# A batched fp32 matmul on one core: the last four batches by halves of the weights, transposes between matmuls, three stores behind the last load

## The chip, the cores and the metric

The kernel runs on one core of one Trainium2 chip. The metric is the device time of one execution in microseconds (us). The profile's span is about 1.8 us shorter than the time of the same execution (525.0 and 526.8 us for the kernel before).

## The reference

```python
def setup_inputs():
    batch, m, k, n = 32, 512, 1024, 768
    return {"x": randn(batch, m, k), "weight": randn(batch, k, n)}   # float32

def reference(x, weight):
    return np.matmul(x, weight).astype(np.float32)
```

Each of the 32 batches reads 2 MB of x and 3 MB of weights, and writes 1.5 MB.

## The kernel before

Engines have the profile's names: PE does the matmuls and the transposes (PEld is its weight loads), DVE is the vector engine, ACT the scalar engine, POOL is GpSimd. PSUM is the memory that PE writes to, and an "evacuation" is the copy of finished outputs from PSUM to SBUF, the core's other memory, from where they are stored. A transfer has "landed" when its semaphore says that it is complete. In the profile's lines x_sb and w_sb are tiles of x and of the weights, pt is a group of transposes in PSUM, xT its copy in SBUF, pm the products in PSUM and out_sb the outputs.

Loads go through GpSimd's queue and cast fp32 to bf16 on the way. PE transposes x (16 transposes of 128x128 pairs per batch, in four groups, one for each tile `mt` of 128 output rows), DVE copies the transposed tiles out of PSUM, and PE multiplies: 64 matmuls per batch, 8 rows of weight tiles (`ko`) times 4 tiles `mt` times 2 column pieces. Most outputs are stored by the Sync engine's queue as soon as they are ready. The parts that matter (cuts are marked `...`):

```python
    KT = K // P                                            # 8 rows of weight tiles
    ...
    N2 = 2 * N                                             # columns of a pair of tiles mt
    CHUNKED = {B - 2: (4, 4), B - 1: (3, 3, 1, 1)}         # load pieces of the last two batches
    HELD = {B - 3, B - 2}                                  # stores put behind the last load
    ...
    xT_pool = ctx.enter_context(tc.tile_pool(name="xT", bufs=6))
    tpsum = ctx.enter_context(tc.tile_pool(name="tpsum", bufs=2, space=bass.MemoryType.PSUM))
    ...
    def load_w(b):
        ws[b] = w_pool.tile([P, KT, N], BF16, name="w_sb")
        at = 0
        for n in CHUNKED.get(b, (KT,)):
            nc.gpsimd.dma_start(out=ws[b][:, at:at + n, :], in_=w_view[b, :, at:at + n, :])
            at += n
    ...
    def evacuate(b, pair, pm):                             # PSUM -> out_sb: 1.0 us ACT, then 0.7 us DVE
        o = outs[b]
        nc.scalar.copy(o[:, pair * N2:pair * N2 + 1024], pm[:, 0:1024])
        nc.vector.tensor_copy(o[:, pair * N2 + 1024:(pair + 1) * N2], pm[:, 1024:N2])
    ...
        for b in range(B):
            if b + 4 < B:
                load_x(b + 4)
                load_w(b + 4)
            outs[b] = out_pool.tile([P, MT * N], F32, name="out_sb")
            if b not in CHUNKED:                           # the "ordinary" order
                xT = {mt: transpose(b, mt) for mt in (0, 1)}
                for pair in range(2):
                    pm = mpsum.tile([P, N2], F32, name="pm")
                    for half in range(2):
                        if pair == 0:
                            matmuls(pm, half, xT[half], b, range(KT), False)
                            xT[2 + half] = transpose(b, 2 + half)
                        else:
                            matmuls(pm, half, xT[2 + half], b, range(KT), False)
                    evacuate(b, pair, pm)
                if b in HELD:
                    continue
                nc.sync.dma_start(out_view[b], outs[b])
            else:                                          # all four transposes in front, then pieces of ko
                xT = {mt: transpose(b, mt) for mt in range(MT)}
                pms = [mpsum.tile([P, N2], F32, name="pm") for _ in range(2)]
                at = 0
                for n in CHUNKED[b]:
                    for mt in range(MT):
                        matmuls(pms[mt // 2], mt % 2, xT[mt], b, range(at, at + n), True)
                        if at + n == KT and mt % 2 == 1:
                            evacuate(b, mt // 2, pms[mt // 2])
                            ...                            # store the pair, unless b is in HELD
                    at += n
            if b == B - 2:
                for h in sorted(HELD):
                    nc.gpsimd.dma_start(out=out_view[h], in_=outs[h])
```

Batches are counted from 0, so the last is batch 31. A "group" of transposes below means the four transposes of one tile `mt`.

## Time and profile before

| | before |
|---|---|
| time, median of the 4 runs beside the changed kernel | 527.17 us (525.1 to 528.21) |
| span of the profiled run | 525.0 us |
| HBM traffic over the span | 415 GB/s |
| last load landed | 504.7 us |
| last matmul ended | 517.8 us |

From the page, the header and three rows of the 40 slices; each digit is a tenth of a slice of 13.1 us, and PEclk is the clock that PE was granted:

```profile
span 525.0 us, 5849 instructions
...
PE   1788879888789878789878798787998878997884
...
PEclk9999999889898989898979989898898989998998
DMA  8999999999999999999999999999999999999982
```

The DMA row is full until the last two slices: for most of the span the loads and stores set the pace, and PE has idle tenths. The last slices are another stage. Here is the chain of waits there (start us, length us, what; the chain is what ended last, followed back):

```profile
471.55 0.95 PE pt L64 x8
472.50 3.66 another core or an unknown queue
...
476.30 4.37 PE pm L78 x16
...
484.22 5.21 PE pm L78 x32
...
489.45 1.02 ACT out_sb L89
...
491.84 1.35 PE pt L64 x8
493.19 10.41 PE pm L78 x64
...
503.62 1.02 ACT out_sb L89
...
506.01 1.35 PE pt L64 x8
507.36 9.76 PE pm L78 x60
```

L78 is the matmul, L64 the transpose. Batch 29 waits 3.66 us for its weights (they land at 476.2; the chain calls the load "an unknown queue"). After that no load appears in the chain: batch 30 starts at 493.19 and batch 31 at 507.36, each after a stretch of about 3.76 us (489.43 to 493.19, 503.60 to 507.36) in which the evacuation, DVE and two rounds of transposes follow one another. PE is behind the loads, and the DMA engines run dry. The windows view shows that, with the two stretches around the wait for batch 29's weights on top. Behind each busy time stands the number of instructions (x); the GB/s count a cast load by its bf16 size (134.59 MB by that count, against 218.1 MB that the page gives for HBM):

```profile
core 0: us, PE busy (x) PEld busy (x) DVE busy (x) ACT busy (x) POOL busy (x), PEclk, DMA share, GB/s
...
472.50:476.20 3.70, 0.00 (x1) 0.00 (x0) 1.89 (x3) 0.10 (x1) 0.00 (x0) 1.00 0.99 214
476.20:479.60 3.40, 3.31 (x11) 1.60 (x12) 0.00 (x0) 0.00 (x0) 0.53 (x1) 0.50 1.01 304
...
505.00:510.00 5.00, 3.99 (x25) 2.80 (x26) 2.85 (x5) 0.00 (x0) 0.53 (x1) 1.00 0.83 347
510.00:515.00 5.00, 5.00 (x33) 3.04 (x32) 0.00 (x0) 0.00 (x0) 0.00 (x0) 1.00 0.15 61
515.00:520.00 5.00, 2.76 (x17) 1.46 (x15) 1.38 (x2) 1.93 (x2) 0.00 (x0) 1.00 0.06 26
```

The DMA share falls to 0.15 and 0.06 while PE still works, and only then are the last 1.5 MB stored. PE idles for 3.7 us from 472.5, and in the 3.4 us after it the granted clock is 0.50: 16 matmuls took 4.37 us there, against 2.60 at full speed.

### The profile page before, as it was taken

How to read it: one execution, taken by the hardware profiler on the slowest of the kernel's cores; microseconds unless marked ns; L12 is line 12 of the kernel's file. 1: busy time of each engine (PE TensorE's matmuls, PEld its weight loads, DVE VectorE, ACT ScalarE, POOL GpSimd, SP SyncE). 2: the span in 40 equal slices, each digit the busy share in tenths (PEclk: the TensorE clock that was granted, in tenths of full speed). 3: DMA queues.
4: the chain of work that ended last, by engine and by line, in shares of the span. 5: the costliest groups of instructions: out<-in, count | busy, mean ns of one | idle time of the engine just before them, and what ended most of it. 6: DMA issues, size and time to landing. Idle time of an engine off the chain costs nothing.

```text
span 525.0 us, 5849 instructions
## 1 busy us (share of the span) xinstructions
PE 431.3 (82%) x2560; PEld 279.3 (53%) x2560; DVE 123.9 (24%) x192; ACT 66.0 (13%) x65; POOL 37.8 (7%) x76
## 2 busy tenths in 40 slices
PE   1788879888789878789878798787998878997884
PEld 1455546555456545455545565454665545664552
DVE  1022221222221212221212212222222212222221
ACT  0001111011110111110101110101110101110011
POOL 4000000000000000000000000000000000000000
PEclk9999999889898989898979989898898989998998
DMA  8999999999999999999999999999999999999982
GB/s 160 215 228 272 271 268 271 277 253 259 263 260 278 261 278 246 265 261 277 262 273 231 273 274 271 274 246 265 258 273 275 254 270 243 274 275 272 214 294 122
DMA packets 14569, 134.59 MB, mean 256 GB/s; under 512 B 1616, under 2 KB 1872, under 8 KB 2640
## 3 DMA queue, kind: packets, MB, share of 16 engines
q0 software_dynamic: 10080, 87.04, 77.6%
q1 hardware_dynamic: 4464, 47.19, 21.7%
q8 instruction: 20, 0.33, 0.2%
q14 instruction: 5, 0.04, 0.0%
HBM read 167.77 MB, written 50.33 MB: 415 GB/s over the span
## 4 chain that ended last, share of the span: by engine, by line
PE 80%; another core or an unknown queue 11%; DMA 3%; ACT 2%; issue 2%; DVE 1%; ACTq 0%; POOL 0%; DVEq 0%; POOLq 0%
PE pm L78 70%; PE pt L64 10%; DMA w_sb<-in_weight_dram 3%; ACT out_sb L89 2%; DVE xT L66 1%; DVE out_sb L90 0%; ACTq L164 0%; POOL x_sb L50 0%; DVEq L66 0%; POOLq L153 0%
## 5 line engine op out<-in xcount | busy, mean ns | idle before, releaser
L78 PE MATMUL pm<-w_sb,xT 128*128 128x256 bf16 (+1 forms) x2048 | 377.0, 344 | 73.8 <-DMA w_sb<-in_weight_dram 63.5
L78 PEld LDWEIGHTS <-xT 128*128 128x128 bf16 x2048 | 208.0, 103 | 218.3 <-issue 61.5
L66 DVE COPY xT<-pt 128x1024 bf16<-128x1024 bf16 x128 | 85.1, 686 | 226.8 <-PE pt L64 226.8
L89 ACT COPY out_sb<-pm 128x1024 f32<-128x1024 f32 x64 | 64.7, 1013 | 452.3 <-PE pm L78 452.3
L64 PE MATMUL pt<-ident,x_sb 128*128 128x128 f32 x512 | 79.7, 291 | 12.6 <-DMA x_sb<-in_x_dram 9.7
L64 PEld LDWEIGHTS pt<-ident,x_sb 128*128 128x128 f32 x512 | 76.6, 207 | 19.8 <-issue 11.9
L90 DVE COPY out_sb<-pm 128x512 f32<-128x512 f32 x64 | 43.9, 686 | 169.1 <-ACT out_sb L89 169.1
L56 POOL DMA_DIRECT2D w_sb<-in_weight_dram x36 | 19.1, 531 | 241.2 <-DMA w_sb<-in_weight_dram 212.4
L50 POOL DMA_DIRECT2D x_sb<-in_x_dram x32 | 17.1, 536 | 198.7 <-PE pt L64 140.6
L138 POOL DMA_DIRECT2D out_dram<-out_sb x2 | 1.1, 534 | 28.1 <-DVE out_sb L90 28.1
L89 ACT ACT_TABLE_LOAD x1 | 1.3, 1283 | 0.7 <-PEq L153 0.7
masks.py:199 POOL TENSOR_SCALAR_AFFINE_SELECT ident<-ident 128x128 f32<-128x128 f32 x1 | 0.3, 287 | 0.1
masks.py:197 POOL MEMSET ident<- 128x128 f32 x1 | 0.2, 243 | 0.0
L153 POOL MEMSET const-float32-0.0<- 128x1 f32 x1 | 0.1, 99 | 0.2 <-issue 0.2
L153 POOL MEMSET const-bfloat16-1.0<- 128x1 bf16 x1 | 0.1, 102 | 0.0
L153 POOL MEMSET const-uint8-127<- 128x1 uint8 x1 | 0.1, 102 | 0.0
L153 POOL MEMSET const-float32-1.0<- 128x1 f32 x1 | 0.1, 99 | 0.0
## 6 DMA issues: line engine op xcount, KB each, us to landing
w_sb<-in_weight_dram POOLq DMA_DIRECT2D x30, 1536.0 KB, 63.1
out_dram<-out_sb SPq DMA_DIRECT2D x29, 1536.0 KB, 14.4
x_sb<-in_x_dram POOLq DMA_DIRECT2D x32, 1024.0 KB, 62.1
out_dram<-out_sb POOLq DMA_DIRECT2D x2, 1536.0 KB, 12.3
w_sb<-in_weight_dram POOLq DMA_DIRECT2D x2, 768.0 KB, 58.3
out_dram<-out_sb SPq DMA_DIRECT2D x2, 768.0 KB, 3.8
w_sb<-in_weight_dram POOLq DMA_DIRECT2D x2, 576.0 KB, 45.6
w_sb<-in_weight_dram POOLq DMA_DIRECT2D x2, 192.0 KB, 32.5
```

Source lines behind the costliest of these rows:

```text
L50: nc.gpsimd.dma_start(out=xs[b], in_=x_view[b])
L56: nc.gpsimd.dma_start(out=ws[b][:, at:at + n, :], in_=w_view[b, :, at:at + n, :])
L64: nc.tensor.transpose(pt[:, j, :], pairs[:, mt, j::JT], ident)
L66: nc.vector.tensor_copy(xT.rearrange("p j m r -> p (j m r)"), pt.bitcast(BF16).rearrange("p j m -> p (j m)"))
L78: nc.tensor.matmul(pm[:, half * N + off:half * N + off + size], xT[:, ko // 2, :, ko % 2], ws[b][:, ko, off:off + size], start=(ko == 0 an ...
L89: nc.scalar.copy(o[:, pair * N2:pair * N2 + 1024], pm[:, 0:1024])
L90: nc.vector.tensor_copy(o[:, pair * N2 + 1024:(pair + 1) * N2], pm[:, 1024:N2])
L138: nc.gpsimd.dma_start(out=out_view[h], in_=outs[h])
L153: nc = _bacc.Bacc("TRN2", target_bir_lowering=False, num_devices=1)
```

## The change

Its intent is to make PE's tail shorter and to use the DMA engines in it. Batches 28 to 31 are loaded and multiplied by halves of the weight rows (the last one by 4, 2, 2). In the second half of a batch, each tile's transposes for the next batch stand in front of that tile's matmuls. Batch 28's store joins the two that wait behind the last load in GpSimd's queue.

```diff
-    CHUNKED = {B - 2: (4, 4), B - 1: (3, 3, 1, 1)}
-    HELD = {B - 3, B - 2}
+    CHUNKED = {B - 4: (4, 4), B - 3: (4, 4), B - 2: (4, 4), B - 1: (4, 2, 2)}
+    HELD = {B - 4, B - 3, B - 2}
...
-    xT_pool = ctx.enter_context(tc.tile_pool(name="xT", bufs=6))
+    xT_pool = ctx.enter_context(tc.tile_pool(name="xT", bufs=8))
...
+        ready = {}
         for b in range(B):
...
-            else:
-                xT = {mt: transpose(b, mt) for mt in range(MT)}
...
+            xT = ready.pop(b, None) or {mt: transpose(b, mt) for mt in range(MT)}
+            pms = [mpsum.tile([P, N2], F32, name="pm") for _ in range(2)]
+            at = 0
+            for n in CHUNKED[b]:
+                last = at + n == KT
+                for mt in range(MT):
+                    if last and b + 1 < B:
+                        ready.setdefault(b + 1, {})[mt] = transpose(b + 1, mt)
+                    matmuls(pms[mt // 2], mt % 2, xT[mt], b, range(at, at + n), True)
+                    if last and mt % 2 == 1:
+                        pair = mt // 2
+                        evacuate(b, pair, pms[pair])
+                        if b not in HELD:
+                            cols = slice(pair * N2, (pair + 1) * N2)
+                            nc.sync.dma_start(out_view[b, :, cols], outs[b][:, cols])
+                at += n
+            if b in HELD:
+                nc.gpsimd.dma_start(out=out_view[b], in_=outs[b])
```

More of the change, by code (lines that the diff above doesn't have):

```diff
@@ L116 @@
                     evacuate(b, pair, pm)
-                if b in HELD:
-                    continue
                 nc.sync.dma_start(out_view[b], outs[b])
-            else:
-                xT = {mt: transpose(b, mt) for mt in range(MT)}
-                pms = [mpsum.tile([P, N2], F32, name="pm") for _ in range(2)]
-                at = 0
-                for n in CHUNKED[b]:
-                    for mt in range(MT):
-                        matmuls(pms[mt // 2], mt % 2, xT[mt], b, range(at, at + n), True)
-                        if at + n == KT and mt % 2 == 1:
-                            evacuate(b, mt // 2, pms[mt // 2])
-                            if b not in HELD:
-                                pair = mt // 2
-                                nc.sync.dma_start(
-                                    out_view[b, :, pair * N2:(pair + 1) * N2],
-                                    outs[b][:, pair * N2:(pair + 1) * N2],
-                                )
-                    at += n
-            if b == B - 2:
-                for h in sorted(HELD):
-                    nc.gpsimd.dma_start(out=out_view[h], in_=outs[h])
+                continue
+            xT = ready.pop(b, None) or {mt: transpose(b, mt) for mt in range(MT)}
[16 more added lines that the diff above has]
+                nc.gpsimd.dma_start(out=out_view[b], in_=outs[b])
 _INS = ['x', 'weight']
```

## The prediction

> **What bounds the kernel now.** Two things, in two stages. For most of the span it is the DMA engines: the slices show them at 9 tenths or more from slice 2 to 38, and the waits list 63.5 us of matmuls waiting for weight loads. The last 50 us differ. In the chain of waits, from the landing of batch 29's weights (476.2 us) to the last matmul (517.4), no load releases the chain: it is PE work, broken by two stretches of 3.7 us (from 489.4, from 503.6) in which the next batch's transposes go through two PSUM buffers and DVE. By the landing records the last weight piece arrives at 504.7. In the windows view the DMA share falls from 1.04 to 0.83 (505 to 510), 0.15 and 0.06 (515 to 520). So about 9 us of DMA time lie unused while PE catches up, and 1.5 MB must still be stored; the span ends 7.6 us after the last matmul.
>
> **What the change does.** Arithmetic and bytes stay.
> 1. Batch 28's store leaves the load stream. Batch 30's loads, with that store beside them, took 16.2 us (landings 476.1 to 492.3); batch 31's, with no store, 12.4. I expect the last load near 501.
> 2. Transposes go between the matmuls of the batch before: batches 29 to 31 lose their 3.6 us stretches and pay four groups of about 0.5 us (four transposes in the chain).
> 3. PE may start on half of the weights: batch 29, which waited until 476.3 for 1.5 MB, can start near 474, behind batch 28.
> 4. The clock records show 3.4 us at half speed from 476.2, just after PE idled from 472.5 to 476.3. The Trainium skill (TensorE: Matmul & The Clock Gate, Part 1) says that an idle window of about 3.4 us throttles PE; this trace agrees. With a dense tail this window, worth 1.7 us, should go.
> 5. The last batch's pair 0 finishes 1.3 us before pair 1, so its evacuations no longer queue: about 1 us.
>
> **Sum.** A batch costs PE 10.4 us of matmuls plus 2.0 of transposes. Batch 28 starts near 461 (its own transposes still stand in front), 29 at 474, 30 at 488 (x of batch 30 lands near 481 and holds its transposes 1.5 us), 31 at 500.5; last matmul near 511 instead of 517.4. Then evacuation 1.8, store issue to landing 4.3, closing 1.0: end near 518. The DMA side gives nearly that: three held stores behind the last load at 3.7 us each (batch 29's store landed 3.7 us after the last load) end near 512, then the last 1.5 MB.
>
> Savings 7 us of 527.36: **520.2 us**, 517.0 to 523.8 (8 in 10). Chances: faster by over 2% 0.09, within 2% 0.90, slower 0.01.
>
> **What would show it.** Chain of waits: no 3.7 us gaps in batches 29 to 31, last matmul near 511. Landings: last load near 501. Windows: DMA share about 1 up to 512. Clock records: no half-speed window between 461 and 511. If the last load lands at 504 or later, step 1 is wrong; if PE still idles over 2 us between batches, step 2 or 3 is.
>
> **What would make it wrong.** The held stores delaying the last 1.5 MB (then the end comes later than 6.5 us after the last matmul); loads in halves moving fewer bytes per us; x of batches 30 and 31 landing late and stopping PE where the transposes now stand.

## The result, and the profile after

| | before | changed |
|---|---|---|
| time, median | 527.17 us (4 runs) | 520.43 us (4 runs, 520.14 to 521.41) |
| ratio to before | | 0.988, 95% interval 0.9847 to 0.9913 |
| span of the profiled run | 525.0 | 518.8 |
| last load landed | 504.7 | 501.1 |
| last held store landed | 513.4 | 512.2 |
| last matmul ended | 517.8 | 512.1 |

A ratio is the mean time of one kernel's fast runs over the mean of the other's of the same rounds, so it is not quite the ratio of the medians quoted. The gain of 1.2% is clear of the noise.

The same rows of the page for the changed kernel, slices of 13.0 us:

```profile
span 518.8 us, 5796 instructions
...
PE   1788789788888878897888978788887879878994
...
PEclk9999899798998979998899989799898997998998
DMA  8999999999999999999999999999999999999996
```

The last slice of the DMA row has gone from 2 tenths to 6, and the one before is full. The chain of waits in the tail:

```profile
465.36 2.83 another core or an unknown queue
...
468.32 1.10 PE pt L64 x4
469.42 2.37 PE pm L78 x8
...
475.82 6.50 PE pm L78 x40
482.32 0.47 PE pt L64 x4
...
488.12 2.71 PE pm L78 x17
...
494.62 0.47 PE pt L64 x4
...
500.42 6.28 PE pm L78 x39
...
506.76 5.38 PE pm L78 x32
512.14 0.02 issue
512.16 1.02 ACT out_sb L89
```

The two stretches of 3.76 us are gone: a group of transposes costs PE 0.47 us between matmuls. A new wait stands at 465.36: in the middle of batch 28, PE waits for x of batch 29, whose transposes now come there; it lands at 468.2. The windows view of the same places:

```profile
core 0: us, PE busy (x) PEld busy (x) DVE busy (x) ACT busy (x) POOL busy (x), PEclk, DMA share, GB/s
465.40:468.30 2.90, 0.00 (x0) 0.01 (x1) 0.00 (x0) 0.00 (x0) 0.00 (x0) 0.96 1.04 327
468.00:471.40 3.40, 3.08 (x11) 1.93 (x12) 0.69 (x1) 0.00 (x0) 0.53 (x1) 0.51 1.05 237
505.00:510.00 5.00, 4.95 (x31) 3.04 (x31) 0.00 (x0) 0.00 (x0) 0.00 (x0) 1.00 0.87 369
510.00:515.00 5.00, 2.12 (x14) 1.08 (x12) 1.38 (x2) 2.02 (x2) 0.00 (x0) 1.00 0.41 168
```

The half-speed stretch has not gone; it has moved from batch 29 to batch 28, behind the new wait. The DMA share from 510 to 515 is 0.41 where it was 0.15.

An account of the 6.2 us between the two spans follows from these chains. Both kernels end batch 29 at the same time, 489.4 (in the changed kernel: 488.12 and eight matmuls of 0.163 us). But in the changed one batch 30's transposes are done by then. From there, before needs twice 3.76 and twice 10.4 us, until 517.8; the changed kernel needs 12.3 (10.4 and four groups of 0.47) and 10.4, until 512.1. That is 5.6 us less; the span then ends 6.7 us after the last matmul instead of 7.3, the other 0.6.

### The profile page after: what moved, and what is told of

Same layout as the page of the kernel before. It is cut to its first block, busy times and chain, and to the rows that moved or that the text cites. A ratio compares the mean times of both kernels' runs of the same rounds, so it can differ in the third digit from the quotient of the medians.

```text
span 518.8 us, 5796 instructions
## 1 busy us (share of the span) xinstructions
PE 425.6 (82%) x2512; PEld 278.3 (54%) x2560; DVE 124.2 (24%) x192; ACT 66.1 (13%) x65; POOL 38.9 (7%) x78
## 4 chain that ended last, share of the span: by engine, by line
PE 80%; another core or an unknown queue 10%; DMA 3%; issue 2%; ACT 2%; DVE 1%; POOL 0%; DVEq 0%; POOLq 0%
PE pm L78 70%; PE pt L64 11%; DMA w_sb<-in_weight_dram 3%; ACT out_sb L89 2%; DVE xT L66 1%; DVE out_sb L90 0%; POOL x_sb L50 0%; DVEq L66 0%; POOLq L152 0%
## 5 line engine op out<-in xcount | busy, mean ns | idle before, releaser
L78 PE MATMUL pm<-w_sb,xT 128*128 128x256 bf16 (+1 forms) x2000 | 372.4, 341 | 72.6 <-DMA w_sb<-in_weight_dram 58.3
L64 PE MATMUL pt<-ident,x_sb 128*128 128x128 f32 x512 | 80.2, 291 | 13.9 <-DMA x_sb<-in_x_dram 12.5
```

The source lines that it names most:

```text
L64: nc.tensor.transpose(pt[:, j, :], pairs[:, mt, j::JT], ident)
L78: nc.tensor.matmul(pm[:, half * N + off:half * N + off + size], xT[:, ko // 2, :, ko % 2], ws[b][:, ko, off:off + size], start=(ko == 0 an ...
```

## The experiments

Theory A is that of the prediction: the gain is PE's shorter tail, and the earlier loads only help a PE that keeps pace with them. Rival B: the gain is the hold, which fills idle DMA time with stores. Rival C: it is the halves, which let PE start early. Every run was correct, and each ratio is against 11 runs of the kernel before on the same chip. There were three chips; before's medians in them were 526.95, 526.94 and 527.05 us.

### The hold alone (e1_hold_only)

```diff
 # the kernel before
-    HELD = {B - 3, B - 2}
+    HELD = {B - 4, B - 3, B - 2}
```

> The kernel before with batch 28's store held too, nothing else. Theory A (the gain is PE's shorter tail; early loads only help a PE that can use them): the last load lands near 501 instead of 504.7, but the last matmul stays near 517 and the time stays within 1.5 us of the kernel before. Rival B (the gain is the hold itself, which fills idle DMA time with stores): 4 to 7 us faster than the kernel before. If PE also gains the start of batch 30, A allows up to 1 us.

Measured: 527.42 us, ratio 1.0005 (0.9982 to 1.0028). The last load landed at 501.0 instead of 504.7, as in the changed kernel, and the last matmul ended at 516.5 in the profiled run, which was the fastest of its six. So loads that come 3.7 us sooner are worth nothing to the old order of PE's work. Rival B falls.

### The hold taken out of the changed kernel (e2_hold_undone)

```diff
 # the changed kernel
-    HELD = {B - 4, B - 3, B - 2}
+    HELD = {B - 3, B - 2}
 ...    # and batch 28's output is stored whole by nc.sync, as before
```

> The changed kernel with batch 28 stored at once as before. Theory A: in the changed kernel x of batches 30 and 31 lands about 1 us before its transposes start, so loads that come 3.6 us later stop PE: last matmul 514 to 515.5 instead of 512.1, time 2 to 3.5 us above the changed kernel's 520.4. Rival B: all of the gain goes, about 527. Rival C (halves and order of PE work are everything): no loss, within 0.8 us of 520.4.

Measured: 523.68 us, ratio 0.9947 (0.9923 to 0.9972), so 3.3 us above the changed kernel; last matmul at 515.1. The same hold that was worth nothing alone is worth half of the gain here. The timeline shows why, PE's instructions with the idle time before each and what ended it:

```profile
482.29 1.13 PE L64 MATMUL pt<-ident,x_sb 128*128 128x128 f32 x4 [2.61 <-DMA x_sb<-in_x_dram]
...
497.32 0.75 PE L64 MATMUL pt<-ident,x_sb 128*128 128x128 f32 x4 [0.98 <-DMA x_sb<-in_x_dram]
```

These are the first transposes of batches 30 and 31, which now wait for x: it lands at 482.2 and at 497.3. In the changed kernel x of batch 31 lands at 493.7.

### The transposes in front again (e3_transposes_front)

```diff
 # the changed kernel
-                    if last and b + 1 < B:
-                        ready.setdefault(b + 1, {})[mt] = transpose(b + 1, mt)
```

> The changed kernel with each batch's four transposes in front of it again. Theory A: batches 29 to 31 pay 3.6 us in front and save 2.0 inside, and batch 28 no longer stops for x of batch 29 (2.9 us): last matmul 514 to 516, time 2 to 4 us above 520.4. Rival B (hold) or C (halves): within 0.8 us of 520.4.

Measured: 522.41 us, ratio 0.9915 (0.9892 to 0.9938): 2.0 us above the changed kernel, at the low edge of what was expected, with the last matmul at 513.1, before the 514 to 516 that were expected. The interleaving is worth 2 us here, not three times the 1.6 us that were charged to it. Without it, batch 28 doesn't stop for x of batch 29 and batch 29's matmuls start at 474.3 instead of 477.1; its own transposes in front fall into a time in which before waits for weights. Only batches 30 and 31 lose by transposes in front.

### Whole loads (e4_whole_loads)

```diff
 # the changed kernel, load_w only
-        for n in CHUNKED.get(b, (KT,)):
+        for n in {B - 1: (4, 2, 2)}.get(b, (KT,)):
```

> The changed kernel with the weights of batches 28 to 30 loaded in one piece each; the order of PE's work is kept. Theory A: in the changed kernel PE starts batches 29 and 30 within 1 us of the second half's landing anyway, so this costs 0 to 1.2 us over 520.4. Rival C (half loads let PE start early): 3 us or more.

Measured: 520.3 us, ratio 0.9873 (0.9852 to 0.9894), the same as the changed kernel. Loading the weights by halves brings nothing when the transposes stand between; rival C, as far as the loads go, falls. (The order of PE's work by halves was kept: it is what makes room for the transposes.)

### The shape of the last batch (e5_tail_3311 and e8_tail_only)

```diff
 # e5: the changed kernel; e8 is the reverse edit in the kernel before
-    B - 1: (4, 2, 2)
+    B - 1: (3, 3, 1, 1)
```

> The changed kernel with the last batch's weights in pieces of 3, 3, 1, 1 rows of tiles as before. Theory A (the shape of the last batch is worth about 1 us: with one tile in the last piece the two pairs end 0.6 us apart and their evacuations queue): the last matmul stays at 512 (within 0.5), the end comes 7.4 to 8 us after it instead of 6.6, time 0.7 to 1.5 us above 520.4. Rival (the shape is worth nothing, because the store waits behind the held stores anyway): within 0.4 us.

> The kernel before with the last batch's weights in pieces of 4, 2, 2, nothing else. Theory A: last matmul unchanged near 517, the end 6.4 to 6.8 us after it instead of 7.6 to 8.0: 0.7 to 1.5 us faster than the kernel before. Rival: within 0.4 us.

Measured: e5 520.79 us, ratio 0.9892 (0.9873 to 0.991), about 0.4 us above the changed kernel; e8 526.5 us, ratio 0.9993 (0.9971 to 1.0015), about 0.4 below before. Neither is clear of the noise. The profiled run of e8 was the slowest of its six, and in it the last matmul ended at 519.3 and not near 517: PE ran at half speed for 6.8 us from 475.6, twice as long as in before's profile. In the profiles the span ends 7.3 us after the last matmul with pieces of one tile row last (before, e5) and 6.6 to 6.7 with two (e8, changed). So the shape is worth about 0.6 us by the traces, and not 1: the two evacuations queue on ACT for 0.35 us only, since one takes 1.01 us and the pairs end 0.65 apart.

### Batch 29's transposes alone in front (e6_front_29)

```diff
 # the changed kernel
-                    if last and b + 1 < B:
+                    if last and b != B - 4 and b + 1 < B:
```

> The changed kernel with only batch 29's transposes in front of it again, so that batch 28 doesn't stop for x of batch 29. Theory A: batch 29's matmuls start near 474.3 (as in the run with all transposes in front) instead of 477.1, no half-speed window at 468, but then x of batch 30 (lands 481.4) stops PE for about 2 us: last matmul near 511.4, time 0.2 to 1.2 us below 520.4. Rival (the stop in batch 28 costs its full 2.9 us plus 1.7 us of half speed): 3 us or more below.

Measured: 520.39 us, ratio 0.9875 (0.9856 to 0.9895), the same as the changed kernel. In this profile there is no half-speed stretch after 449, batch 28 doesn't stop, and PE then waits for x of batch 30 (until 481.5) all the same; the last matmul ends at 511.9. So the wait and the half-speed stretch in batch 28 cost the changed kernel next to nothing: PE gives the time back at the next landing of x.

### A fourth held store (e7_hold_four)

```diff
 # the changed kernel
-    HELD = {B - 4, B - 3, B - 2}
+    HELD = {B - 5, B - 4, B - 3, B - 2}
 ...
-                nc.sync.dma_start(out_view[b], outs[b])
+                if b in HELD:
+                    nc.gpsimd.dma_start(out=out_view[b], in_=outs[b])
+                else:
+                    nc.sync.dma_start(out_view[b], outs[b])
                 continue
```

> The changed kernel with batch 27's store held too. Theory A (with the dense tail PE runs within 1 us of the loads, so earlier loads are now worth time, until the DMA's own end binds): last load near 497.4, no stop for x of batch 29, last matmul 508 to 509.5; four held stores end near 512.2 as three did, and the last 1.5 MB behind them: end near 517, time 1.2 to 2.2 us below 520.4. Rival (PE alone binds, the loads have slack): within 0.5 us of 520.4.

Measured: 518.91 us (518.57 to 519.03), ratio 0.9848 (0.9827 to 0.987). Each of its five runs is below all eight of the changed kernel. This version beats both kernels. Last load 497.3, last matmul 507.8, last held store 512.6, last store 516.1. One expectation missed: batch 28 still stops for x of batch 29, for 0.8 us. Two lines of the windows view:

```profile
505.00:510.00 5.00, 2.75 (x17) 1.46 (x15) 1.38 (x2) 2.02 (x2) 0.00 (x0) 0.98 0.92 391
510.00:515.00 5.00, 0.00 (x0) 0.00 (x0) 0.00 (x0) 0.00 (x0) 0.00 (x0) 0.50 0.72 300
```

From 510 on PE has nothing left to do and the DMA share is 0.72, where it was 0.41. The end now comes 9.4 us after the last matmul, and the two last stores take 6.3 us from issue to landing where they took 3.5: held stores and the last output follow each other, at about 3.7 us for 1.5 MB, and set the end.

### Two further corners: transposes in front with two and with four held stores (e9_front_hold_two, e10_front_hold_four)

```diff
 # e9: e2 (two stores held), e10: e7 (four stores held); in both
-                    if last and b + 1 < B:
-                        ready.setdefault(b + 1, {})[mt] = transpose(b + 1, mt)
```

> The changed kernel with the transposes in front again and batch 28 stored at once: both main parts undone, only the halves and the last batch's shape left. Theory A (the hold only pays when PE keeps pace with the loads; with transposes in front PE is slower than the loads): the hold is worth nothing here, time 521.8 to 523.4, like the 522.4 of the run with transposes in front and the hold, and not slower than the 523.7 with the transposes between and no hold. Rival (the two parts add): 522.4 + 3.2 = 525.6, within 1 us.

> Transposes in front, but four stores held. Theory A: last load near 497.4 and no gain, since PE binds: 521.6 to 523.2, against the 518.9 of four held stores with the transposes between. Rival (each held store gives 1.5 us or more anyway): 521 or less.

Measured: e9 522.8 us, ratio 0.9916 (0.9899 to 0.9932); e10 522.0 us, ratio 0.9914 (0.9892 to 0.9936). With these the table is full (medians, ratios to before in brackets):

| | two stores held | three | four |
|---|---|---|---|
| transposes in front | 522.8 (0.9916) | 522.4 (0.9915) | 522.0 (0.9914) |
| transposes between | 523.7 (0.9947) | 520.4 (0.988) | 518.9 (0.9848) |

The columns and rows come from different chips; each ratio is to before. In the first row the hold is worth nothing. In the second, each held store is worth time. With two held, the transposes between are even slower than in front (the intervals, 0.9899 to 0.9932 and 0.9923 to 0.9972, still overlap a little; the medians differ by 0.9 us). Neither part brings its gain alone, and the sum of effects measured one at a time would mislead. But the largest part of the gain needs neither: with both undone (e9) the kernel is still 0.8% faster than before, about two thirds of the 1.2%. What that rests on, e12 shows below.

The traces tell what sets the end of PE's work in each row. With the transposes in front, the last matmul follows the start of batch 29's matmuls by a fixed time, 38.8 us (three batches of 10.4 and two stretches of 3.76): 474.3 and 513.1 both in e3 and in e10, although x of batch 31 lands at 493.6 in one and at 489.9 in the other. There PE paces itself, and earlier loads wait for it. The timelines of e3 and, below, of e10 (the recorded start of a group overlaps the one before by 0.16 us):

```profile
474.14 10.56 PE L78 MATMUL pm<-w_sb,xT 128*128 128x512 bf16 x62
502.49 10.56 PE L78 MATMUL pm<-w_sb,xT 128*128 128x512 bf16 x62
...
474.14 10.56 PE L78 MATMUL pm<-w_sb,xT 128*128 128x512 bf16 x64
502.50 10.56 PE L78 MATMUL pm<-w_sb,xT 128*128 128x512 bf16 x64
```

With the transposes between, the last matmul follows the landing of batch 31's x by a fixed time: 497.3 and 515.1 (e2), 494.1 and 511.9 (e6), 489.9 and 507.8 (e7), each 17.8 us, about the PE work of half a batch with four groups of transposes and a whole batch (5.2, 1.9 and 10.4). That does not show that this landing is the bound. Only e2 waits for it (0.98 us). The last wait of PE for a load is in e6 the one for x of batch 30, and in e7 the one for x of batch 29; from then on PE works without a stop that the timeline shows, and comes to x of batch 31 within 0.2 us of its landing. The timeline of e7:

```profile
465.36 0.72 PE L64 MATMUL pt<-ident,x_sb 128*128 128x128 f32 x4 [0.82 <-DMA x_sb<-in_x_dram]
...
477.75 0.63 PE L64 MATMUL pt<-ident,x_sb 128*128 128x128 f32 x4
...
490.05 0.67 PE L64 MATMUL pt<-ident,x_sb 128*128 128x128 f32 x4
```

A batch with the next one's transposes costs PE 12.3 us, and with three or four stores held x of batch 31 lands 12.2 to 12.6 us after x of batch 30 (12.5 in e7, and there x of batch 30 lands 12.2 after that of batch 29). So PE is at the loads' pace; the end keeps its distance to several landings, and these runs don't tell which of them it would follow alone.

### The changed kernel again, and batch 28 in the ordinary order (e11_changed_again, e12_batch28_ordinary)

```diff
 # e12: the changed kernel
-    CHUNKED = {B - 4: (4, 4), B - 3: (4, 4), B - 2: (4, 4), B - 1: (4, 2, 2)}
-    HELD = {B - 4, B - 3, B - 2}
+    CHUNKED = {B - 3: (4, 4), B - 2: (4, 4), B - 1: (4, 2, 2)}
+    HELD = {B - 3, B - 2}
 ...
-                    if last and b + 1 < B:
-                        ready.setdefault(b + 1, {})[mt] = transpose(b + 1, mt)
```

> The changed kernel itself, once more, as the measure for the others of this call: 520.0 to 521.4, ratio 0.986 to 0.989. In some of its runs a half-speed window falls into batch 28 and in others not; if the loads set the pace, that makes less than 1 us.

> As the first run of this call (transposes in front, two stores held), but batch 28 in the ordinary order, so that only batches 29 to 31 run by halves. Theory A (what the halves bring is that batch 28's four transposes run while PE would wait for its weights, and that batch 29 doesn't wait for all of its weights): batch 29's matmuls start 0.5 to 2.5 us later than in that run, time 522.5 to 525.5. Rival (the order of batch 28 doesn't matter): the same as that run within 0.5 us.

Measured: e11 520.86 us (519.87 to 521.27), ratio 0.9878 (0.9859 to 0.9897), which repeats the 0.988. In its profile no half-speed stretch falls into the tail, and its last matmul follows x of batch 31 by 17.8 us (493.6 to 511.4); in the first profile of the changed kernel it was 18.4 (493.7 to 512.1). The other profiles with three held stores and the transposes between agree: 18.4 in e4, which has a half-speed stretch from 468.4, and 17.8 to 17.9 in e5 and e6, which have none. So the half-speed stretch, with the longer stop before it, is worth about 0.6 us.

This second profile differs from the first in where PE waits. Here x of batch 29 lands at 466.3, before PE asks for it, and PE waits for x of batch 30:

```profile
467.54 0.63 PE L64 MATMUL pt<-ident,x_sb 128*128 128x128 f32 x4
...
481.29 0.75 PE L64 MATMUL pt<-ident,x_sb 128*128 128x128 f32 x4 [1.29 <-DMA x_sb<-in_x_dram]
...
493.71 0.64 PE L64 MATMUL pt<-ident,x_sb 128*128 128x128 f32 x4
```

Batch 29's matmuls start at 474.8, while the second half of its weights lands at 476.4.

e12: 522.73 us, ratio 0.9926 (0.9908 to 0.9945), like e9; its batch 29 starts at 475.5, in e9 at 476.1. What I expected of batch 28's order didn't come: it matters less than the noise of about 1 us. But e12 is a small edit of the kernel before (batch 29 by halves with its four transposes in front, the last batch's shape, and a larger pool for transposed tiles), and it is already 4 us faster. The windows around batch 29's start, to be held against the two of before:

```profile
472.50:476.20 3.70, 2.23 (x16) 1.63 (x15) 3.15 (x5) 0.27 (x1) 0.53 (x1) 1.00 1.04 217
476.20:479.60 3.40, 3.40 (x23) 2.10 (x22) 0.02 (x1) 0.00 (x0) 0.00 (x0) 1.00 1.01 303
```

In before PE was idle in the first of these and at a clock of 0.50 in the second. Here the second two of the four groups of transposes fall into the first, matmuls start at 475.5, and the second runs at full clock. Batch 29's matmuls end at 485.9 instead of 489.4: 0.8 us from the earlier start, 1.8 from the clock (4.37 against 2.60 us for the first 16 matmuls), and 0.95 because two groups no longer stand inside the batch. The runs don't separate these three by the time itself. The larger pool was not tried alone. Nor was e12 tried with whole loads: its batch 29 starts before the second half of its weights has landed (476.5), so that what e4 says of the halves need not hold here.

## Why the prediction was right

The predicted time was 520.2 us, the measured 520.4. The time was right because the sum carried the right constraint: that x of the next batch, and not its weights, would hold PE where the transposes now stand. The second profile (e11) ran as the sum has it: batches 29, 30 and 31 start at 474.8, 488.7 and 501.0 (474, 488 and 500.5 were said), x of batch 30 holds PE for 1.3 us (1.5), and the last matmul ends at 511.4 (511). The first did not: there x of batch 29 held PE for 2.8 us, x of batch 30 (481.3) was there before PE came at 482.3, and the last matmul ended at 512.1. Point by point, by the first profile where no other is named:

- **The bound.** Right. The tail was PE's, with idle DMA time. e1 shows it: loads 3.7 us earlier and no gain.
- **Step 1, the hold.** Right in the landing (501.1 against "near 501"). The Trainium skill (DMA: Bandwidth & Descriptors, "Issuing engines are not separate DMA queues") says that DMAs of all issuers interleave on the same 16 engines. With batch 28's store on the Sync queue beside them (e2), the loads of the last batches land 3.6 us later. What the prediction did not say is that the hold is worth something only with the interleaving, and the interleaving only with the hold.
- **Step 2, the transposes.** Right in mechanism, wrong in count. "batches 29 to 31 lose their 3.6 us stretches": batch 29 had none to lose, since its stretch lay in a wait for weights. Two of 3.76 us went, for 1.9 us of transposes between matmuls in place of them: 5.6 us. Against transposes in front with three stores held (e3), the interleaving is worth 2.0 us.
- **Step 3, starting on half of the weights.** It failed in the first profile and came true in the second (474.8, e11); the two runs took 520.6 and 519.9 us. In the first, batch 29 started at 477.1 and not at 474, as batch 28 stopped 2.8 us for x of batch 29 (I had taken its landing of before, 466.7; it came at 468.2). Whole loads cost nothing (e4). Nor was the later start worth anything: PE has to wait for x of batch 30 if it starts earlier (e6, e11). With the transposes in front it is another matter: there what changes at batch 29 makes up most of the gain (3.5 us between the profiles of before and e12).
- **Step 4, the half-speed stretch.** Wrong as a forecast for the first profile: there was one, from 468.0; in the second there was none. It followed the new wait as the old one had followed the old wait. Its worth was put at 1.7 us and was about 0.6 by five profiles (e11), because without it PE waits for x of batch 30.
- **Step 5, the last batch's shape.** Mis-sized: about 1 us was put, the traces show 0.6, the times 0.4, not clear of noise.
- **The tail.** Last matmul at 512.1, "near 511" was said; the end came 6.7 us after it, and over 6.5 was named as the sign of delay by the held stores. The two last stores took 3.5 us from issue to landing (median), against 3.8 before, so nothing was delayed. The DMA share did not stay at 1 until 512: it was 0.87 from 505 to 510. Why it dips there is not settled.

In the first profile two misses lay on opposite sides: batch 29 started 3.1 us later than said, and the 1.5 us for x of batch 30 fell away, since PE came after it. That is not luck alone, because being late uses up the next wait. That it cancels so closely rests on PE's 12.3 us for a batch being so near the 12.4 us between the landings of x of batches 30 and 31; the prediction did not say so.

## What to carry to other kernels

When a stage is bound by a chain on one engine and, a little below that, by the arrival of its inputs, removing either alone gives little or nothing; try the parts together, and fill in the whole table before giving a gain to one of them. Look in the traces for the event that the end follows at a fixed distance (here PE's own start plus 38.8 us, or the landing of the last x plus 17.8), and then whether anything really waits for that event: where two things run at the same pace, the end keeps its distance to both. Hold stores back behind the last load while PE can use the earlier loads; here four were better than three, and five were not tried. And look at what a change brings with its two main ideas taken out: here that was two thirds of the gain.

## What the Trainium skill lacked or had wrong

- "TensorE: Matmul & The Clock Gate", Part 1, says that PE is throttled after an idle window of about 3.4 us. In the changed kernel a stop of 2.96 us was enough (465.36 to 468.32, with a half-speed record from 468.05), and in before one of 1.99 us (to 444.2, record from 445.5); in another run of the changed kernel PE didn't stop at 465 and no half-speed record followed. The page does say that the window runs freely; it does not say how much shorter than a window a stop may be. Before's trace, cut into these windows of 3.41 us, gives a border: each full-speed window in which PE was busy with matmuls and transposes for 1.42 us or less was followed by a half-speed one, none with 1.66 us or more was; over all 14 profiles the border lies between 1.38 and 1.48 us. The half-speed records of one run start at whole multiples of 3.41 us from each other (76.8, 93.9, 445.5, 476.2 in before), which agrees with the page.
- "DMA: Bandwidth & Descriptors", "Where 436 GB/s comes from", says that for transfers between HBM and SBUF the HBM side binds at about 358 GB/s. That sentence gives no condition; the page itself says a few lines above, under its measurements, that this is the share when both cores of the pair stream. With this one core at work, HBM reads and writes came to 415 GB/s over the span of before and 420 over that of the changed kernel; held stores took 3.6 to 3.8 us for 1.5 MB, 1.57 million bytes, 3.7 in the mean, some 425 GB/s. The 425 GB/s for 16 MB that the same section quotes fits better.
- No page that I read says that the whole time of a kernel on one core can follow the granted clock from run to run. Of the 33 runs of the kernel before, the 8 at or below 525.61 us had a mean granted clock of 0.937 or 0.938, and the 14 at or above 527.23 us one of 0.934 or 0.935. The eight runs of the changed kernel show no such order: its slowest, 521.41 us, has a clock of 0.942, the highest of the eight. That the half-speed stretches are the cause in before is argued and not shown.
